# When the expert weights of blocks 1 to 4 are spread out: one number in the order of a hybrid layer

## The chip, the cores and the metric

One core of a Trainium2 chip runs the whole kernel. The metric is the device time of one execution in microseconds (us). A core has engines that work side by side, each in the order of its own instruction list: TensorE (PE in the profile, its weight loads PEld), VectorE (DVE), ScalarE (ACT), GpSimd (POOL), and SyncE (SP), which issues most transfers. Sixteen DMA engines move the data; the transfers that SP, ACT and POOL issue share them.

## The reference, cut to what matters

One layer over 1024 tokens of 1024 numbers (float32). A mixing part (an RWKV-7 recurrence and a latent attention, both gated) is added to x. Then comes PEER, a choice among 16384 experts, and then a gated embedding and a norm:

```
x  += (sigmoid(gate_A) * yA + sigmoid(gate_B) * yB) @ W_out
h2  = rms_norm(x)
# PEER: 8 heads x 16 experts = 128 (index, gate) pairs per token
top_s, top_i = top_k(h2 @ w_q against two sets of 128 keys, 16)   # per head
idx, gate    = the 16 best of the 256 pairs, softmax of their scores
act = gelu(sum_d h2[t, d] * u_tab[idx[t, k], d])                  # 128 dots per token
x  += sum_k gate[t, k] * act[t, k] * v_tab[idx[t, k]]
x  += sigmoid(rms_norm(x) @ W_pg) * (p @ W_ple)
out = rms_norm(x)
```

## The kernel before, in words

The 1024 tokens are eight blocks of 128, and two blocks are a slice (0 to 3). For each slice there is a projection, the recurrence (`rwkv`), the rest of the projection, attention (`attend`), and the choice (`select`): `select` joins the two branches, adds them to x, computes the queries, multiplies them with the keys, and `combine` makes 128 indices and gates for each token of a block.

PEER then has two ways for the sum over v:

- **Dots, all blocks** (`gather`): for each of a block's 128 columns, POOL issues an indirect DMA (L907) that fetches one row of u for each of the 128 tokens (128 rows of 4 KB), and VectorE multiplies it with h2 and sums (L909). Four row buffers are there, seven after `more_rows`. At the end the gates are multiplied by gelu of the dots.
- **Blocks 5, 6, 7** (`add_rows`): the same with rows of v (L922), which VectorE scales and adds to x (L924).
- **Blocks 0 to 4** (`expand`, `dense`): the gates are spread into a full table W, 16384 experts by 128 tokens, and all of v is multiplied with it. `expand_block` splits each index into its upper and lower seven bits, transposes both and the gates, and makes for each token two columns: `oa` (VectorE, L966: where iota equals the upper part, the gate) and `ob` (ScalarE, L961 and L962). TensorE multiplies them (L968), four tokens to a bank of PSUM; ScalarE copies the bank to `ws` (L969); after 64 tokens, half a block, SP issues four writes of 1 MB to W in DRAM (L971). `dense` reads W (L989) and v (L999), splits each number into two parts for a faster matmul form (L282 on ScalarE, L284 on VectorE) and runs 3840 matmuls (L1003 to L1005) for the five blocks together, adding into x by L1008. It can't begin before every block of W is written.

At last `ple` does the gated embedding and the final norm, block by block in the order 0 to 7.

The order on the engines is made by a planner when the kernel is built. Each call in `everything` carries a number; every instruction traced in that call gets it as its priority. The planner follows a modelled time and gives an idle engine, of the instructions that are ready and whose buffers are free, the one with the lowest number. The order so found is fixed: on the chip each engine takes its list in order and waits where an operand is not there yet. So a number does not say when a call runs, only who goes first where two are ready. The part of the list that matters here:

```
(11.2, self.project_rwkv, 3), (10.5, self.attend, 2), (11, self.select, 2), (51, self.gather, [4]),
(49, self.expand, [0]), (16.1, self.rwkv, 3), (15, self.project_rest, 3), (49.5, self.attend, 3), (52.5, self.select, 3),
(52, self.gather, [5]), (49, self.expand, [1, 2, 3, 4]), (60, self.ple_weights, 0), (53, self.more_rows, None),
(53, self.gather, [6, 7]), (50, self.dense, 0),
(56, self.add_rows, 5), (57, self.add_rows, 6), (58, self.add_rows, 7),
(60, self.ple, range(8)),
```

Memory follows the order of the calls as they are written: `expand` of 1 to 4 has its buffers on the right side, where those of `rwkv` 3 lay before, so it can start when that is done. `attend` 3 and `select` 3 lie on the left side. The buffers of `dense` and the three more row buffers lie where theirs and the streamed weights' lay.

Of the kernel before, what the change touches and what calls it, by code (L numbers as in the profile page):

```python
# [151 lines left out]
class Program:  # L152
# [912 lines left out]
    def everything(self):  # L1065
        nc = self.nc
        order = [
            (0, self.project_rwkv, 0), (0.1, self.rwkv, 0), (0.2, self.project_rest, 0), (1, self.attend, 0),
            (1.5, self.select, 0), (50, self.gather, [0, 1]), (2, self.project_rwkv, 1), 
            (4.9, self.rwkv, 1), (5, self.project_rest, 1), (5.2, self.project_rwkv, 2), (5.5, self.attend, 1), (6, self.select, 1),  # L1070
            (50, self.gather, [2, 3]),
            (11.1, self.rwkv, 2), (10, self.project_rest, 2), 
            (11.2, self.project_rwkv, 3), (10.5, self.attend, 2), (11, self.select, 2), (51, self.gather, [4]),
            (49, self.expand, [0]), (16.1, self.rwkv, 3), (15, self.project_rest, 3), (49.5, self.attend, 3), (52.5, self.select, 3),
            (52, self.gather, [5]), (49, self.expand, [1, 2, 3, 4]), (60, self.ple_weights, 0), (53, self.more_rows, None),
            (53, self.gather, [6, 7]), (50, self.dense, 0),
            (56, self.add_rows, 5), (57, self.add_rows, 6), (58, self.add_rows, 7),
            (60, self.ple, range(8)),
        ]
        with ExitStack() as st:  # L1080
            self.kp = self.pool(self.ctx, "cx", "right")
            self.wp = self.pool(st, "wts", "left")
            begun = {}
            self.tc.cur_priority = PHASE // 20
            self.rope_tables()
            for prio, f, a in order:
                if f == self.more_rows:
                    st.close()
                    self.xp = self.pool(self.ctx, "dx", "left")
                    self.gp2 = self.pool(self.ctx, "rows", "left")  # L1090
                    continue
                self.tc.cur_priority = int(prio * PHASE)
                self.aux = nc.gpsimd if f == self.rwkv else nc.vector
                if f == self.project_rwkv:
                    begun[a] = f(a)
                elif f == self.attend:
                    f(a)
                    if a + 1 in begun:
                        begun[a + 1][1].close()
                elif f == self.project_rest:  # L1100
                    begun[a][1].close()
                    f(a, begun[a])
                elif f == self.ple_weights:
                    f("right")
                else:
                    f(a)
# [15 lines left out]
```

## Time and profile before

| what | value |
|---|---|
| median of 3 runs | 3807.69 us (3803.22 to 3827.1) |
| the profiled execution | 3820.92 us, its span 3819.2 us |
| mean granted clock of TensorE in it | 0.886 |
| VectorE, TensorE busy over the span | 81%, 81% |
| moved by DMA | 1160.34 MB, mean 304 GB/s |

Times in the profile count from the span's start. A row of the view of stretches gives the stretch and its length, then the busy time of each engine with its number of instructions, the granted clock of TensorE (1.00 is full), the DMA engines' mean share, and GB/s; asked for one line alone, it has that line's engines only. A row of a timeline gives start, duration, engine, line, operation, output and inputs, the count of like ones merged, and in brackets the idle time before it with what ended it. A row of waits has who waited for whom, the total, how often, and the longest. A row of the chain of work that ended last gives start, duration and what it was.

### The profile page before, as it was taken

To read this page: it belongs to the slowest core of one execution; us is meant where nothing else is said; L and a number is where in the kernel's file an instruction comes from. 1 tells how busy PE (TensorE), PEld (TensorE's weight loads), DVE (VectorE), ACT (ScalarE), POOL (GpSimd) and SP (SyncE) were. 2 spreads that over 40 slices of the span, in tenths; PEclk is the share of its full clock that TensorE was granted. 3 is DMA by queue.
4 is the path that set the end of the run, shared out by engine and by line. 5 is a ranking of instruction groups with operands and counts; after the bars stand their busy time and mean duration, and the time that the engine had idled before them with its cause. 6 is when DMAs were issued, how large, how long until landed. Compare 5 with 4: busy or idle time off the path is not lost. (4 is left out here: it accounts for less than half of the span.)

```text
span 3819.2 us, 60838 instructions
## 1 busy us (share of the span) xinstructions
PE 3111.7 (81%) x21423; PEld 2470.6 (65%) x21423; DVE 3089.1 (81%) x6864; ACT 1299.5 (34%) x2821; POOL 1869.7 (49%) x1502
## 2 busy tenths in 40 slices
PE   6998688768999886698966787737889889888988
PEld 6885677656588774467843566636767667776743
DVE  4632689766789777789978877989999999999996
ACT  4432322124122148311226866642222222222244
POOL 2210355555433543454455433326767766666674
PEclk9998889779999898698977788858999999999999
DMA  6335498889887998998998999889999999999995
GB/s 206 98 92 176 134 342 308 287 300 335 314 290 275 321 334 268 306 355 299 339 290 282 298 336 322 276 305 369 374 384 376 383 374 379 376 367 384 363 331 208
DMA packets 494705, 1160.34 MB, mean 304 GB/s; under 512 B 47680, under 2 KB 222016, under 8 KB 494400
## 3 DMA queue, kind: packets, MB, share of 16 engines
q0 software_dynamic: 202752, 738.29, 53.7%
q1 hardware_dynamic: 274368, 402.42, 30.7%
q10 hardware_dynamic: 17280, 15.74, 1.2%
q8 instruction: 170, 2.79, 0.3%
q14 instruction: 135, 1.11, 0.1%
HBM read 1071.33 MB, written 84.93 MB: 303 GB/s over the span
## 5 line engine op out<-in xcount | busy, mean ns | idle before, releaser
L907 POOL DMA_INDIRECT u<-in_u_dram,idx x1024 | 1229.2, 1200 | 1307.9 <-DVE dots L909 686.9
L909 DVE CUSTOM_DVE_ANT_0 u<-u,gh 128x1024 f32<-128x1024 f32 x1024 | 1243.4, 1225 | 240.6 <-DMA u<-in_u_dram,idx 230.5
L922 POOL DMA_INDIRECT u<-in_v_dram,idx x384 | 496.0, 1292 | 230.0 <-DVE x L924 115.7
L1004 PE MATMUL acc<-vlo,Whi 128*128 128x512 f32 x1280 | 522.3, 408 | 69.2 <-DVE vlo L284 68.5
L1005 PE MATMUL acc<-vhi,Wlo 128*128 128x512 f32 x1280 | 514.4, 402 | 0.0
L1003 PE MATMUL acc<-vhi,Whi 128*128 128x512 f32 x1280 | 369.4, 401 | 95.8 <-DMA vr<-in_v_dram 42.2
L292 PE MATMUL mm<-hT,w 128*128 128x128 f32 x3456 | 418.6, 282 | 3.2 <-ACT z L332 1.7
L292 PEld LDWEIGHTS mm<-hT,w 128*128 128x128 f32 x3456 | 408.6, 197 | 16.4 <-issue 6.0
L1003 PEld LDWEIGHTS acc<-vhi,Whi 128*128 128x128 f32 x1280 | 243.7, 192 | 171.0 <-ACT vhi L282 87.0
L1004 PEld LDWEIGHTS acc<-vlo,Whi 128*128 128x128 f32 x1280 | 249.3, 195 | 146.9 <-DVE vlo L284 95.9
L292 PE MATMUL mm<-act,w 128*128 128x256 f32 x1280 | 315.7, 403 | 28.8 <-DVE gate L779 11.9
L282 ACT ACTIVATE vhi<-vr 128x512 fp32r<-128x512 f32 x256 | 158.0, 628 | 521.6 <-DMA vr<-in_v_dram 378.6
L924 DVE SCALAR_TENSOR_TENSOR x<-u,gate,x 128x1024 f32<-128x1024 f32 x256 | 328.1, 1282 | 6.5 <-DMA u<-in_v_dram,idx 2.3
L968 PE MATMUL w<-ob,oa 128*128 128x128 f32 x1280 | 224.2, 336 | 94.3 <-ACT ob L962 52.6
L292 PEld LDWEIGHTS mm<-act,w 128*128 128x128 f32 x1280 | 252.1, 202 | 70.2 <-DVE gate L779 13.5
L1005 PEld LDWEIGHTS acc<-vhi,Wlo 128*128 128x128 f32 x1280 | 249.7, 195 | 51.6
L968 PEld LDWEIGHTS w<-ob,oa 128*128 128x128 f32 x1280 | 205.4, 243 | 117.6 <-ACT ob L962 79.8
L966 DVE TENSOR_SCALAR oa<-cst,pt 128x128 f32<-128x128 f32 x640 | 186.8, 353 | 40.4 <-PE w L968 37.2
L961 ACT ACTIVATE ob<-cst,pt 128x128 f32<-128x128 f32 x640 | 204.0, 392 | 1.2 <-PE w L968 1.1
L284 POOL TENSOR_TENSOR wlo<-w,whi 128x1024 fp32r<-128x1024 f32 x26 | 63.8, 2452 | 257.5 <-ACT whi L282 239.2
L282 ACT ACTIVATE Whi<-wr 128x1280 fp32r<-128x1280 f32 x64 | 81.5, 1273 | 317.7 <-PE acc L1004 268.3
L284 DVE TENSOR_TENSOR vlo<-vr,vhi 128x512 fp32r<-128x512 f32 x256 | 171.9, 685 | 2.8 <-ACT vhi L282 2.6
(308 smaller groups left out, 5259.3 us busy)
## 6 DMA issues: line engine op xcount, KB each, us to landing
w<-in_w_in_dram SPq DMA_DIRECT2D x144, 512.0 KB
vr<-in_v_dram SPq DMA_DIRECT2D x256, 256.0 KB
W<-ws SPq DMA_DIRECT2D x40, 1024.0 KB
wr<-W SPq DMA_DIRECT2D x64, 640.0 KB
w<-in_w_q_dram SPq DMA_DIRECT2D x64, 512.0 KB
w<-in_w_out_dram SPq DMA_DIRECT2D x32, 512.0 KB
u<-in_u_dram,idx POOLq DMA_INDIRECT x1024, 7.1
x<-in_x_dram SPq DMA_DIRECT2D x16, 512.0 KB
```

The costliest lines, as they stand in the source:

```text
L282: self.nc.scalar.activation(act[0], x, AF.Copy)
L284: (lo_engine or self.aux).tensor_tensor(act[1], x, act[0], op=OP.subtract)
L292: mm(ps, w[0][:, i], a[0][:, i], start=first, stop=last)
L907: nc.gpsimd.indirect_dma_start(out=u[:], out_offset=None, in_=self.I["u"], in_offset=bass.IndirectOffsetOnAxis(ap=idx[:, k:k + 1], axis=0))
L909: nc.vector.tensor_tensor_reduce(out=u[:], in0=u[:], in1=h[:], scale=1.0, scalar=0.0, op0=OP.mult, op1=OP.add, accum_out=dots[:, k:k + 1])
L922: nc.gpsimd.indirect_dma_start(out=v[:], out_offset=None, in_=self.I["v"], in_offset=bass.IndirectOffsetOnAxis(ap=idx[:, k:k + 1], axis=0))
L924: nc.vector.scalar_tensor_tensor(x, v, gate[:, k:k + 1], x, op0=OP.mult, op1=OP.add)
L961: nc.scalar.activation(c[:, i], self.c("iota"), AF.Abs, bias=pt[:, 1, k + i:k + i + 1])
L968: nc.tensor.matmul(ps[:, i], a, c[:, i], start=True, stop=True)
L1003: nc.tensor.matmul(acc[b], wh, vh, start=i == 0, stop=False)
L1004: nc.tensor.matmul(acc[b], wh, vl, start=False, stop=False)
L1005: nc.tensor.matmul(acc[b], wl, vh, start=False, stop=i == G - 1)
```

## The change

One number in the order. The call that expands blocks 1 to 4 had 49, lower than attention 3, the gathers of blocks 4 and 5 and choice 3; it gets 52.8, higher than those and lower than the 53 of the gathers of blocks 6 and 7. The expansion of block 0 and the dense product keep theirs.

```
-            (52, self.gather, [5]), (49, self.expand, [1, 2, 3, 4]), (60, self.ple_weights, 0), (53, self.more_rows, None),
+            (52, self.gather, [5]), (52.8, self.expand, [1, 2, 3, 4]), (60, self.ple_weights, 0), (53, self.more_rows, None),
```

## The prediction

> **What bounds the kernel now.** First the page: span and shares.
>
> ```profile
> span 3819.2 us, 60838 instructions
> PE 3111.7 (81%) x21423; PEld 2470.6 (65%) x21423; DVE 3089.1 (81%) x6864; ACT 1299.5 (34%) x2821; POOL 1869.7 (49%) x1502
> ```
>
> No engine is full over the whole span, so the stages have to be taken apart. The view by stretches does that (busy us of PE, PEld, DVE, ACT, POOL, each with its count; then granted clock, DMA share, GB/s):
>
> ```profile
> 2050.00:2460.00 410.00, 309.33 (x1572) 247.26 (x1571) 334.58 (x1000) 287.34 (x757) 165.32 (x144) 0.84 0.92 309
> 2460.00:2530.00 70.00, 43.73 (x184) 38.01 (x184) 69.90 (x293) 53.22 (x135) 19.16 (x17) 0.59 0.78 259
> 2560.00:3640.00 1080.00, 940.10 (x3840) 735.39 (x3840) 1015.20 (x1299) 241.10 (x330) 725.08 (x548) 0.96 0.99 374
> 3640.00:3819.00 179.00, 154.12 (x400) 67.82 (x400) 145.09 (x209) 73.33 (x154) 101.52 (x78) 0.94 0.74 265
> ```
>
> From 2050 to 2530 three things share the engines: attention and choice of the last slice, the expansion of blocks 1 to 4, and the gathers of blocks 4 and 5. VectorE is busy 82% and then 100%, the DMA 92% and then 78%. From 2560 to 3640 the dense product runs beside the gathers of blocks 6 and 7 and the added rows; VectorE has 94%, the DMA 99%. After 3640 the output stage fills TensorE. Where that stage hands over is read from the timelines of SP, PE, POOL and DVE:
>
> ```profile
> 2111.38 17.66 SPq L971 DMA_DIRECT2D W<-ws  x4
> ...
> 2483.94 15.83 SPq L971 DMA_DIRECT2D W<-ws  x4
> ...
> 2530.51 18.63 SPq L971 DMA_DIRECT2D W<-ws  x4
> 2564.56 0.81 SPq L989 DMA_DIRECT2D wr<-W  x2
> ...
> 2572.08 2.50 PE L1003 MATMUL acc<-vhi,Whi 128*128 128x512 f32 x5 [42.23 <-DMA vr<-in_v_dram]
> ...
> 2585.39 0.20 DVE L876 CAST idx<-idf 128x64 int32<-128x64 f32 x1
> 2587.00 1.68 POOL L907 DMA_INDIRECT u<-in_u_dram,idx  x1 [28.15 <-DVE dots L909]
> ...
> 3643.44 0.66 PE L254 MATMUL tr<-cst,p 128*128 128x128 f32 x2 [8.57 <-DMA p<-in_p_dram]
> ...
> 3781.80 1.28 DVE L924 SCALAR_TENSOR_TENSOR gh<-u,gate,gh 128x1024 f32<-128x1024 f32 x1
> ```
>
> Two chains meet at the end. **The TensorE chain**: the last half block of the expansion is written from 2530.5, read back at 2564.6, the dense product starts at 2572.1 and ends at 3643.4 - 8.6 = 3634.9 (1063 us), and the output stage takes 3643.4 to 3819.2 = 176 us, of which TensorE works 154. **The row chain**: block 7's indices are ready at 2585.6, the last row is added at 3783.1, and 36 us later the last block is out. Both are late together: cutting one alone brings almost nothing, delaying either one costs.
>
> **The change part by part.** Only a number changes, 49 to 52.8. Nothing is added or removed: the same 640 columns (512 of them here), the same 32 writes of W. What the scheduler chose first on each engine, the expansion, now comes behind attention 3 (49.5), the dots of blocks 4 and 5 (51, 52) and choice 3 (52.5); the gathers of 6 and 7 (53) stay behind it. The dense product (50) still can't start before the last W is written. So the question is when the expansion ends.
>
> *What it needs.* The view of stretches, for each of its lines alone (columns made on DVE; then its three ACT steps):
>
> ```profile
> 2050.00:2530.00 480.00, 149.53 (x512) 0.80 0.90 301
> 2050.00:2530.00 480.00, 162.58 (x511) 0.80 0.90 301
> 2050.00:2530.00 480.00, 76.76 (x128) 0.80 0.90 301
> 2050.00:2530.00 480.00, 75.08 (x128) 0.80 0.90 301
> ```
>
> ScalarE needs 163 + 77 + 75 = 314 us, VectorE 150, of 480. At the front it takes (2530.5 - 2111.4) / 7 = 59.9 us per half block; the last half, when the choice's matmuls are over, takes 2530.5 - 2483.9 = 46.6.
>
> *Its pace when it is behind.* Block 0's expansion shows it: that call (49) stood behind attention 2 (10.5), and it ran in that stage's gaps:
>
> ```profile
> 1457.79 16.29 SPq L971 DMA_DIRECT2D W<-ws  x4
> ...
> 1527.49 16.73 SPq L971 DMA_DIRECT2D W<-ws  x4
> ```
>
> That is 69.7 us per half. So "behind" doesn't mean "after": ACT is free enough to be filled.
>
> *How long it is behind.* The choice's product with the keys, in stretches of 20 us, first and last of slice 2 (no expansion beside it) and of slice 3:
>
> ```profile
> 1680.00:1700.00 20.00, 1.22 (x8) 1.21 (x8) 0.90 0.94 337
> ...
> 1760.00:1780.00 20.00, 0.71 (x4) 0.52 (x4) 0.81 0.75 235
> ...
> 2340.00:2360.00 20.00, 0.61 (x4) 0.60 (x4) 1.00 0.97 324
> ...
> 2440.00:2460.00 20.00, 3.91 (x16) 3.38 (x16) 0.70 0.60 178
> ```
>
> That is some 80 us against 120. SP is the queue that both share: a half block's four writes hold it for 14 to 18 us, and loads wait in order behind them:
>
> ```profile
> 2420.52 16.99 SPq L971 DMA_DIRECT2D W<-ws  x4
> 2437.61 9.85 SPq L817 DMA_DIRECT2D keys<-in_keys_dram  x4
> ...
> POOL u L907 <- DVE dots L909: 124.5, 48, 13.4
> POOL u L907 <- DVE oa L966: 110.3, 66, 9.4
> ```
>
> My estimate is that the choice ends at 2400 instead of 2460 (40 us for the key loop, 20 for SP). Until then 350 us / 70 = 5.0 halves; the other 3.0 at 50 us (46.6, and a little for the rows of block 6 beside them) end at 2550: **20 us later** than 2530. Bounds: all eight at 69.7 gives 2608 (+78); on the other side VectorE did 335 + 70 us of work in 480, so without a gap the same work could be through 75 us earlier (-75). I take +20 because the nearest row, block 0, is a filler beside the same kind of stage.
>
> *What is queued behind.* On VectorE a column of the expansion now stands behind dots that wait for their row; the matmuls of L968, the copies on ACT and the writes on SP wait with it. The call's small steps (index split, three transposes, their copies, once a block) move along; on POOL it issues nothing. The eight times four writes cost nothing after the choice, because then SP has only the load of one block of h and the dense product's loads, which need them anyway; if a load of the choice is still behind them, that is 17 us each time. In exchange the rows no longer wait 110 us behind columns (the POOL row above). Their rate (L907 alone, count in brackets):
>
> ```profile
> 700.00:800.00 100.00, 56.13 (x45) 0.74 0.82 281
> 2133.00:2515.00 382.00, 144.72 (x125) 0.82 0.92 311
> ```
>
> 33 rows per 100 us there, 45 where no expansion runs. At 45, block 5 takes 284 us instead of 382 and ends at 2417. Block 6 starts then and not at 2531; by a dense start of 2592 some 75 rows are through. Before, it was 14 when the product began (first and last of 14 rows), and 78 of the 640 stood behind its end:
>
> ```profile
> 2531.19 1.44 POOL L907 DMA_INDIRECT u<-in_u_dram,idx  x1 [17.14 <-DVE idx L876]
> ...
> 2557.91 0.94 POOL L907 DMA_INDIRECT u<-in_u_dram,idx  x1 [0.30 <-issue]
> ...
> 3640.00:3780.00 140.00, 101.52 (x78) 0.96 0.93 331
> ...
> 3801.98 6.98 PE mm L292 x16
> ```
>
> So 640 - 14 - 78 = 548 rows went beside 1063 us of product, 1.94 us each; the lead of 61 rows is worth about 118 us on the row chain.
>
> *What is late next.* That lead is hidden by the TensorE chain: of 565 rows still to come at 2592, 548 fit beside the product as they do now, so its 1063 us stay. It ends at 3655, and the output stage then waits for next to no added row. Of its 176 us TensorE idles 22; 10 stand behind the last matmul (3801.98 + 6.98, the chain's last row above), of the rest I take 8. **Sum: +20 - 8 = +12 us.**
>
> The profiled execution took 3820.9 (span 3819.2), 13 above the median of 3807.7 (3803 to 3827). The difference is put on the median: **3820 us**.
>
> **The rivals.**
> 1. *The rows set the pace of the dense product (faster).* For it: DMA 0.99 at 374 GB/s throughout. 61 rows of 128 x 4 KB are 32 MB, 86 us at that rate. If that bandwidth passes to the loads of v and W, the product shortens by it: 20 - 8 - 86 = -74, **3734**; half of it gives **3777**. TensorE has room: two matmuls of a full run start 0.23 us apart, 3840 x 0.23 = 883 of 1063 us.
>
> ```profile
> 2580.04 0.39 PE L1004 MATMUL acc<-vlo,Whi 128*128 128x512 f32 x1
> 2580.27 0.39 PE L1005 MATMUL acc<-vhi,Wlo 128*128 128x512 f32 x1
> ...
> ACT vhi L282 <- DMA vr<-in_v_dram: 378.6, 132, 9.6
> PE acc L1004 <- DVE vlo L284: 65.3, 51, 3.4
> ```
>
>    Against it: TensorE itself waits for VectorE (65 us), and as long as rows remain, POOL takes up what is freed. Chance 0.20. The Trainium skill ("DMA: Bandwidth & Descriptors", Specifications) puts HBM at about 358 GB/s per core; the 374 here lies a little above, and by that rule the stage is full and this rival is the case. The same page (Measured) has 425 GB/s for one core with its neighbour idle; by that one it is not full. No run here tells the two apart yet.
> 2. *The columns starve behind dots (slower).* Dots whose rows are late hold VectorE in order. If a half takes 90 us until 2400, 3.9 are done, 4.1 x 50 follow: 2605, +75 - 8 = +67, **3875**. It decides from a pace of about 78 us per half on. Against it: columns need 150 of 480 us. Chance 0.26.
> 3. *Really last (slower).* All eight halves after the choice, at 46.6: 2400 + 373 = 2773, +243 - 8: **4043**. Block 0 speaks against it. Chance 0.03.
> 4. *It does nothing.* The gaps were already what the expansion ran in, the order hardly moves: **3808**, give or take 10. Chance 0.08.
>
> **How the numbers follow.** The forecast has 0.43; its own range, from -10 to +45, is the uncertainty of the choice's end and of 50 us per half. The range 3765 to 3885 takes in forecast, rival 4, most of rival 2 and the nearer part of rival 1; about 0.19 is left out. One per cent, 38 us, is about what a measurement of this kernel can tell from none. Faster by more: rival 1 and a little of the forecast, 0.22. Slower by more: rivals 2 and 3 and the edge of the forecast, 0.31. Within: 0.47.
>
> **What would show it.** Right: W's last writes near 2550 and the first dense matmul near 2590; keys done near 2400; block 6's rows beginning some 100 us before the dense product; the dense product still about 1060 us; the last added row well before 3783 while TensorE is full from the end of the dense product to the end. Wrong: a dense product clearly under 1030 us (rival 1), W's last writes after 2590 (rivals 2, 3) or before 2520; or an added row that is still last.

## The result, and the profile after

| kernel | median | runs |
|---|---|---|
| before, same chip | 3809.31 us | 4 |
| after | 3854.89 us (3847.81 to 3856.91) | 4 |

The ratio is 1.0108, 95% interval 1.0085 to 1.0131: slower by about 1%. The profiled execution of after took 3856.91 us, its span is 3855.1; against the span before, 3819.2, that is +35.9. The medians are 46 apart; the pieces below are those of the two profiled executions. Forecast was +12.

First the page's span, and the view by stretches (PE, PEld, DVE, ACT, POOL, then granted clock, DMA share, GB/s) of the kernel after:

```profile
span 3855.1 us, 60828 instructions
...
2050.00:2460.00 410.00, 306.40 (x1508) 242.72 (x1507) 344.57 (x1040) 271.24 (x702) 174.70 (x153) 0.82 0.93 312
2460.00:2530.00 70.00, 41.19 (x185) 36.77 (x186) 66.73 (x285) 55.88 (x144) 16.50 (x17) 0.62 0.85 289
2530.00:2600.00 70.00, 20.61 (x72) 15.98 (x71) 64.20 (x148) 21.67 (x52) 44.61 (x34) 0.52 0.93 319
2600.00:3675.00 1075.00, 934.80 (x3811) 732.29 (x3812) 995.55 (x1241) 236.87 (x323) 709.97 (x542) 0.95 0.98 372
3675.00:3855.00 180.00, 157.85 (x430) 72.42 (x428) 123.65 (x196) 76.76 (x162) 67.73 (x57) 0.96 0.56 203
```

There is a new stretch, 2530 to 2600, in which TensorE does 21 us of 70: the dense product would have begun here, but W isn't complete. Up to 2460 ScalarE did less than before (271 us against 287) and VectorE more (345 against 335). At the other end the output stage has 57 rows beside it, not 78. The handovers, from the timelines of SP, PE, POOL and DVE:

```profile
2344.07 16.64 SPq L971 DMA_DIRECT2D W<-ws  x4
2461.17 24.12 SPq L971 DMA_DIRECT2D W<-ws  x4
2510.95 19.09 SPq L971 DMA_DIRECT2D W<-ws  x4
2566.87 17.05 SPq L971 DMA_DIRECT2D W<-ws  x3
...
2604.73 0.81 SPq L989 DMA_DIRECT2D wr<-W  x2
...
2612.17 2.50 PE L1003 MATMUL acc<-vhi,Whi 128*128 128x512 f32 x5 [45.96 <-DMA vr<-in_v_dram]
...
2508.35 1.44 POOL L907 DMA_INDIRECT u<-in_u_dram,idx  x1 [12.59 <-DVE idx L876]
...
3689.19 0.66 PE L254 MATMUL tr<-cst,p 128*128 128x128 f32 x2 [7.43 <-DMA p<-in_p_dram]
...
3780.64 1.27 DVE L924 SCALAR_TENSOR_TENSOR gh<-u,gate,gh 128x1024 f32<-128x1024 f32 x1
```

Piece by piece along the TensorE chain:

| piece | before | after | difference |
|---|---|---|---|
| dense product starts | 2572.1 | 2612.2 | **+40.1** |
| dense product, its length | 1062.8 | 1069.6 | +6.8 |
| gap to the output stage | 8.6 | 7.4 | -1.1 |
| output stage | 175.8 | 165.9 | **-9.9** |
| span | 3819.2 | 3855.1 | +35.9 |

So the loss is the late start of the dense product. The fifth half block is written from 2344.07, as before (2344.73); the sixth from 2461.17 instead of 2420.52, 117 us after the fifth and not 76; the last from 2566.87 instead of 2530.51. The columns of the expansion alone (L966 on VectorE) show the place, first of the kernel before, then of the one after:

```profile
2050.00:2340.00 290.00, 93.11 (x319) 0.81 0.92 311
2340.00:2400.00 60.00, 13.96 (x49) 0.94 0.94 322
2400.00:2460.00 60.00, 15.49 (x52) 0.86 0.86 281
2460.00:2530.00 70.00, 26.96 (x92) 0.59 0.78 259
```

```profile
2050.00:2340.00 290.00, 94.25 (x324) 0.82 0.94 316
2340.00:2400.00 60.00, 7.87 (x25) 0.94 0.99 347
2400.00:2460.00 60.00, 10.99 (x35) 0.75 0.80 256
2460.00:2530.00 70.00, 27.32 (x94) 0.62 0.85 289
2530.00:2600.00 70.00, 10.51 (x34) 0.52 0.93 319
```

For 290 us the number in the order changed next to nothing in the columns done: 319 and 324. In the 120 us around the choice's product with the keys (its key loop) there are 60 columns where there were 101. Those 41 are missing; 7 more in the stretches around it make up for a part, and 34 come behind 2530. What took their place, by VectorE's groups between 2340 and 2460 (count | busy us, mean ns | idle before), before and after:

```profile
L909 DVE CUSTOM_DVE_ANT_0 u<-u,gh 128x1024 f32<-128x1024 f32 x41 | 49.4, 1213 | 3.1 <-DMA u<-in_u_dram,idx 3.1
L966 DVE TENSOR_SCALAR oa<-cst,pt 128x128 f32<-128x128 f32 x101 | 29.5, 350 | 7.0 <-PE w L968 6.9
L832 DVE FIND_INDEX8 ti<-ts,s 128x8 uint32<-128x128 f32 x28 | 7.7, 284 | 0.0
```

```profile
L909 DVE CUSTOM_DVE_ANT_0 u<-u,gh 128x1024 f32<-128x1024 f32 x48 | 57.9, 1210 | 0.1
L966 DVE TENSOR_SCALAR oa<-cst,pt 128x128 f32<-128x128 f32 x60 | 18.9, 355 | 4.7 <-PE w L968 4.5
...
L832 DVE FIND_INDEX8 ti<-ts,s 128x8 uint32<-128x128 f32 x32 | 8.8, 284 | 0.0
```

Seven more dots and the rest of the choice's searches (32 of each of the five kinds, L831 to L835, where there were 24 to 30) stand for 41 columns, which are 10.6 us of VectorE. VectorE was busy 104 of these 120 us before and 110 after, so it is not its time that ran out. What changed is its list. Counted in the order of its instructions in the trace, 118 columns stand between the choice's first and last search (L831 to L835) in the kernel before, and 50 in the kernel after; the dots between them are nearly as many, 44 and 40. The columns that stood among the searches went behind them. At 2460 the expansion is 36 columns behind (420 done before, 384 after), some 26 us at 46.6 us per half block; the rest then goes a little slower, 52 us per half, and the last column is 38 us late (2527.1 and 2565.1). The waits in the same stretch, before and after:

```profile
PE w L968 <- ACT ob L962: 4.7, 2, 3.2
```

```profile
PE w L968 <- DVE oa L966: 19.9, 9, 9.9
```

Before, the matmuls of the expansion waited in this stretch now and then for ScalarE's columns and never for VectorE's. After, they waited for VectorE's, up to 9.9 us at a time (and 6.2 us in all for ScalarE's). ScalarE was busy 72 us of these 120 before and 52 after, so it wasn't short of time. That the columns which came late held up the four-token steps behind them is read from these lists and waits; no kernel changed VectorE's list alone.

### The profile page after: what moved, and what is told of

Read it like the earlier page. It is cut to its first block, busy times and chain, and to the rows that moved or that the text cites. A ratio compares the mean times of both kernels' runs of the same rounds, so it can differ in the third digit from the quotient of the medians.

```text
span 3855.1 us, 60828 instructions
## 1 busy us (share of the span) xinstructions
PE 3106.8 (81%) x21423; PEld 2468.7 (64%) x21423; DVE 3093.8 (80%) x6864; ACT 1302.2 (34%) x2821; POOL 1852.4 (48%) x1502
## 4 chain that ended last, share of the span: by engine, by line
PE 23%; issue 23%; DVE 21%; DMA 15%; POOL 12%; ACT 4%; SPq 1%; POOLq 0%; DVEq 0%; ACTq 0%
DMA u<-in_u_dram,idx 9%; POOL u L907 8%; DVE u L909 8%; PE mm L292 8%; POOL u L922 3%; DVE oa L966 2%; PE mm L788 2%; PE acc L1004 2%; PE acc L1005 1%; PE w L968 1%; PE acc L1003 1%; PE inv L589 1%; PE mm L294 1%; PE S L738 1%; PE mm L295 1%
## 5 line engine op out<-in xcount | busy, mean ns | idle before, releaser
L907 POOL DMA_INDIRECT u<-in_u_dram,idx x1024 | 1221.4, 1193 | 1320.8 <-DVE dots L909 669.3
L922 POOL DMA_INDIRECT u<-in_v_dram,idx x384 | 486.5, 1267 | 238.5 <-DVE x L924 114.2
L968 PE MATMUL w<-ob,oa 128*128 128x128 f32 x1280 | 241.0, 348 | 132.8 <-DVE oa L966 65.1
L968 PEld LDWEIGHTS w<-ob,oa 128*128 128x128 f32 x1280 | 216.1, 251 | 163.5 <-ACT ob L962 85.2
L966 DVE TENSOR_SCALAR oa<-cst,pt 128x128 f32<-128x128 f32 x640 | 188.4, 354 | 43.1 <-PE w L968 41.0
```

What stands on the lines that cost most here:

```text
L907: nc.gpsimd.indirect_dma_start(out=u[:], out_offset=None, in_=self.I["u"], in_offset=bass.IndirectOffsetOnAxis(ap=idx[:, k:k + 1], axis=0))
L922: nc.gpsimd.indirect_dma_start(out=v[:], out_offset=None, in_=self.I["v"], in_offset=bass.IndirectOffsetOnAxis(ap=idx[:, k:k + 1], axis=0))
L966: nc.vector.tensor_scalar(a, self.c("iota"), pt[:, 0, k:k + 1], pt[:, 2, k:k + 1], op0=OP.is_equal, op1=OP.mult)
L968: nc.tensor.matmul(ps[:, i], a, c[:, i], start=True, stop=True)
```

## The experiments

In the first three sections **theory A** is: to be behind the choice, in its key loop, costs the expansion the 41 columns. **Rivals**: being behind the dots of block 5; or a loss wherever it is behind anything. In the two sections on rows, theory A and its rival are about another question, the prediction's first rival: do the rows set the dense product's length?

### Behind the dots of block 5 only

```
-            (52, self.gather, [5]), (49, self.expand, [1, 2, 3, 4]),
+            (52, self.gather, [5]), (52.3, self.expand, [1, 2, 3, 4]),
```

> The expansion of blocks 1 to 4 at 52.3: behind attention 3 and the dots of blocks 4 and 5, still in front of choice 3 (52.5). Theory A, the choice's key loop is what takes VectorE from the expansion: then nothing is lost here, 3809 give or take 12, W's last writes near 2530 as before. Theory B, the dots of block 5 are what starves the columns: most of the 46 us are lost here, 3840 to 3860, W's last writes near 2570.

Measured: 3824.2 us beside 3816.22, ratio 1.0018 (1.0002 to 1.0034). SP's and PE's timelines:

```profile
2418.68 17.26 SPq L971 DMA_DIRECT2D W<-ws  x4
...
2566.82 2.50 PE L1003 MATMUL acc<-vhi,Whi 128*128 128x512 f32 x5 [39.76 <-DMA vr<-in_v_dram]
```

The sixth half is as early as before (2420.52), the dense product starts 5 us earlier. To stand behind attention and both blocks' dots costs the start nothing. The time lies 3 us above theory A's range, beside a kernel before that took 3816 here and not 3809; theory B's 3840 is far off.

### The choice first, everything else as before

```
-  (49.5, self.attend, 3), (52.5, self.select, 3),
+  (49.5, self.attend, 3), (48.9, self.select, 3),
```

> The expansion stays at 49, choice 3 goes from 52.5 to 48.9: the choice alone passes in front of it (and of the dots of blocks 4 and 5). Theory A (the choice's key loop takes VectorE from the expansion): the dense product starts 25 to 45 us later than before, near 2600 to 2615, and the time is 3835 to 3860. Theory B (the dots do it): the dense product starts where it did, 2572, and the time is 3795 to 3815.

Measured: 3846.76, ratio 1.0082 (1.0057 to 1.0107).

```profile
2457.68 16.00 SPq L971 DMA_DIRECT2D W<-ws  x4
...
2598.46 2.50 PE L1003 MATMUL acc<-vhi,Whi 128*128 128x512 f32 x5 [44.63 <-ACT vhi L282]
```

Here the dots stay behind the expansion and the choice is ahead of it (48.9 is also ahead of attention 3 and of the dots, so theirs is not quite the old place), and the sixth half is 37 us late, the dense product 26. The choice suffices for most of the loss; behind attention and the dots alone the start is not late.

### Blocks 1 and 2 behind, or blocks 3 and 4, or block 4 alone

```
             for b in blocks:
+                self.tc.cur_priority = int((52.8 if 0 < b < 3 else 49) * PHASE) + 5000 * b
                 self.expand_block(b, pool, psum, len(blocks) > 1)
```

with `0 < b < 3`, `b > 2` and `b == 4` for the three.

> Only blocks 1 and 2 of the expansion at 52.8, blocks 3 and 4 at 49. Theory A, the loss is all made in the last three halves, when the key loop runs: 3809 give or take 12, as before. Rival, the loss is spread evenly over the eight halves: 3825 to 3840.

> Blocks 1 and 2 at 49, blocks 3 and 4 of the expansion at 52.8. Theory A, the loss is all made in the last three halves: the full loss, 3845 to 3860, the dense product starting near 2610. Rival, the loss is spread evenly: 3825 to 3840.

> Blocks 1, 2 and 3 of the expansion ahead of the choice as in the kernel before, block 4 alone behind it. Theory A (only the halves that are still to be done in the choice's key loop, 2340 to 2460, lose): the sixth half, block 3's second, keeps its place and its writes start near 2420 as before, block 4's first half loses the 20 to 40 us of the key loop that are left: 3815 to 3835, W's last writes between 2530 and 2555. Rival (what counts is that the last block of the expansion lies behind the choice, wherever it is then): the full loss, 3845 to 3860.

| behind the choice | median | ratio |
|---|---|---|
| blocks 1, 2 | 3805.33 | 0.9974 (0.9953 to 0.9996) |
| blocks 3, 4 | 3854.77 | 1.0105 (1.0080 to 1.0130) |
| block 4 | 3824.41 | 1.0020 (1.0000 to 1.0040) |

The kernel before took 3816.22 beside the first two and 3817.87 beside the third. SP's and PE's timelines of the kernels with blocks 1 and 2, with 3 and 4, and with 4 behind:

```profile
2508.71 11.50 SPq L971 DMA_DIRECT2D W<-ws  x4
...
2539.76 2.50 PE L1003 MATMUL acc<-vhi,Whi 128*128 128x512 f32 x5 [31.70 <-ACT vhi L282]
```

```profile
2461.69 23.21 SPq L971 DMA_DIRECT2D W<-ws  x4
...
2609.58 2.50 PE L1003 MATMUL acc<-vhi,Whi 128*128 128x512 f32 x5 [45.95 <-ACT vhi L282]
```

```profile
2414.11 17.21 SPq L971 DMA_DIRECT2D W<-ws  x4
2486.82 14.25 SPq L971 DMA_DIRECT2D W<-ws  x4
...
2578.73 2.50 PE L1003 MATMUL acc<-vhi,Whi 128*128 128x512 f32 x5 [44.54 <-ACT vhi L282]
```

All three times are in theory A's ranges. Blocks 3 and 4 carry the whole of the loss, with the sixth half (block 3's second) at 2461.69 as in the kernel after. With block 4 alone behind, the sixth half keeps its place, the seventh is 3 us late and the start 7. So it matters which halves stand behind, those that are due in the key loop; and a block 4 that comes behind the choice when that is nearly over loses little.

The kernel with blocks 1 and 2 behind was a little faster than the kernel before. It was run once more:

> The same kernel as first_two_behind (blocks 1 and 2 behind the choice, 3 and 4 ahead of it), with more rounds, since its gain (0.9974) is small. If the gain is the earlier end of W (dense product from 2540 instead of 2572, with both chains ending 18 us earlier in the profile): 3795 to 3810 and a ratio of 0.995 to 0.999. If it was chance: 1.000 within 0.002.

Measured: 3811.27 beside 3817.87, ratio 0.9978 (0.9959 to 0.9997). The small gain is there twice, but it is well under the 1% that the prediction takes as what a measurement of this kernel can tell from none. Its dense product starts 32 and 24 us before that of the kernel before, but lasts 14 and 18 us longer in its two profiles. Why its W is complete earlier wasn't settled.

### Fewer rows beside the dense product

Block 7's dots for 64 of 128 columns, in the kernels before and after:

```
-            for k in range(128):
+            for k in range(64 if b == 7 else 128):
```

With it one small VectorE instruction in every block's `gather` sets the second half of `dots` to zero.

> The kernel before, but block 7's dots are taken for 64 of its 128 columns only; the other 64 dots are set to zero. That leaves out 64 fetched rows of u (64 x 0.52 MB) and their products, all of which lie beside the dense product. It measures how much the rows set the dense product's length. Theory A (TensorE's own chain sets the product; the rows only fill the transfers beside it): the product stays within 20 us of 1063, and the time is 3790 to 3815, the little gain being the output stage that no longer waits for the last blocks. Rival B (the transfers set it; 64 x 0.52 MB at 374 GB/s are 90 us): the product shrinks to 970 to 990, and the time is 3720 to 3745. In between, in proportion.

> The same removal of 64 columns of block 7's dots (64 rows of u left out), on the changed kernel, whose dense product starts 40 us later. Theory A: 3835 to 3855, the distance to the same removal on the kernel before stays at 35 to 45 us, since the late start of the dense product is passed on whole. Rival B (transfers set the pace): 3765 to 3790 with a distance that may be smaller, since the rows that the changed kernel has fetched ahead count there.

Measured: 3784.45, ratio 0.9928 (0.9903 to 0.9953), and 3838.47, ratio 1.0075 (1.0054 to 1.0097). The first lies 6 us below theory A's range, the second in it; both are far from the rival. But the profile shows that the edit was no test of it. The view by stretches of the first one, for its dense product and its output stage:

```profile
2545.00:3614.00 1069.00, 943.97 (x3840) 738.65 (x3839) 1010.40 (x1236) 236.15 (x323) 714.03 (x542) 0.95 0.99 372
3614.00:3788.00 174.00, 151.19 (x400) 67.29 (x400) 89.40 (x166) 76.05 (x161) 31.72 (x27) 0.95 0.33 121
```

POOL issued 542 rows beside 1069 us of product; before, 546 beside 1063. The rows of v moved up, and most of the 64 are missing from the output stage (27 rows, not 78). So the transfers beside the product were never fewer. The 30 us gained are for the most part another thing: the dense product started at 2545, 27 us earlier. The row fetches that were left out lie behind that start, but seven of the eight small instructions that set the dots to zero lie ahead of it, and the planner found another order: VectorE's list differs otherwise too from 2135 us on, and 136 columns stand among the choice's searches where 118 stood. In the two kernels with 64 rows less the starts are 50 us apart and the times 54, more than the 35 to 45 that theory A expected.

The start also varies with no change of the order. In the kernel before and the two kernels of the next section the lists of VectorE, ScalarE and GpSimd are the same up to 3318 us, and the dense product starts at 2572, 2560 and 2561; in the two profiles of the kernel with blocks 1 and 2 behind it starts at 2540 and 2548. So a difference of some 12 us between single profiles says nothing, and the verdict on the choice rests on all kernels together. In the four in which blocks 3 and 4 stand behind the choice (after, choice first, blocks 3 and 4 behind, and after with 64 rows less) 47 to 56 columns stand among its searches, and the dense product starts between 2595 and 2612. In the other nine it is 93 to 136 columns, and a start between 2535 and 2579.

### No rows in the last third of the dense product

The kernel before; blocks 6 and 7 add 8 of 128 rows of v, once with neither fetch nor addition of the rest, once with all additions but no fetch:

```
             for k in range(128):
+                if b > 5 and k >= 8:
+                    break
```

```
             for k in range(128):
-                v = self.row(); (indirect fetch of the row)
+                if b == 5 or k < 8:
+                    v = self.row(); (indirect fetch of the row)
```

> The kernel before, but blocks 6 and 7 add only 8 of their 128 rows of v: 240 rows are neither fetched nor added. So the last third of the dense product (from about 3300) has no rows beside it, which the removal of 64 rows of u did not bring: there the rows behind them moved up, 542 instead of 546 beside the product. In 200 us of the product there are now 720 to 764 matmuls. Theory A (TensorE's own chain, rows only fill): the same 720 to 770 in the stretches without rows, and 3795 to 3810 in all. Rival (rows take from the product, by transfers or by VectorE): 850 or more in those stretches, the product 40 to 60 us shorter, 3740 to 3770 in all.

> The same 240 rows of v are not fetched, but VectorE still does all 240 additions (with a row that is already there), 1.27 us each. It separates what the rows take: if their transfers do, the product's pace in the stretches without fetches rises as in the kernel that has neither (850 or more matmuls in 200 us), and the time is within 15 us of that one. If VectorE's additions do, the pace stays at 720 to 770 while they run, and the time is 3790 to 3815.

Measured: 3754.59, ratio 0.9847 (0.9815 to 0.9880), and 3811.68, ratio 0.9998 (0.9979 to 1.0018). One stretch of 220 us well inside the product, of the kernel before, then without fetch and addition, then with the additions alone:

```profile
3340.00:3560.00 220.00, 195.57 (x813) 153.50 (x813) 213.18 (x216) 48.82 (x67) 145.00 (x115) 0.98 0.99 375
```

```profile
3340.00:3560.00 220.00, 220.00 (x973) 182.16 (x972) 89.16 (x120) 58.21 (x80) 0.00 (x0) 1.00 0.36 117
```

```profile
3340.00:3560.00 220.00, 207.67 (x907) 169.00 (x906) 220.00 (x231) 54.97 (x75) 0.00 (x0) 1.00 0.35 110
```

Without rows TensorE is busy for the whole 220 us and does 973 matmuls, 20% more than the 813 beside rows (0.226 us each against 0.271; the granted clock, 1.00 against 0.98, can be 2% of it). With the transfers gone and VectorE still full it does 907. So of the 160 matmuls that the rows cost, 94 come back when the transfers go and 66 more when the additions go too; fetches without additions were not run, so the shares hold for this order only. Theory A in its strict form, that rows only fill, is wrong: they slow the product. The whole product took 1030 and 1046 us instead of 1063: 33 us less without rows, where the rival had said 40 to 60. The second kernel's total, 3811.68, is no faster because the additions reach into the output stage, which lasts 199 us instead of 176: from 3600 to 3700 VectorE is busy 99 us and TensorE 72. The Trainium skill ("DMA: Bandwidth & Descriptors", Specifications) puts HBM at about 358 GB/s per core; by that a stretch at 375 is full and transfers set its pace. The trace agrees in part: at 110 GB/s the pace rose by 12%, and VectorE, busy all 220 us, held it from there. That the stretch was full at 375 is not shown by it.

### The writes of W from two queues

```
-                nc.sync.dma_start(self.W[part][q]...
+                (nc.scalar if q % 2 else nc.sync).dma_start(self.W[part][q]...
```

in the kernel before, and in the one with blocks 1 and 2 behind.

> The kernel before, with the four writes of each half block of W issued in turn by SyncE and ScalarE instead of all by SyncE. It measures whether the holding of SyncE's queue by the writes (14 to 19 us for four, 78.8 us for eight in the changed kernel) is a part of the way from the last column of W (2526.8) to the first read (2564.6). If it is: the dense product starts 5 to 12 us earlier and the time is 3803 to 3812. If only the landing of the writes counts: 3812 to 3822, no difference. If ScalarE, which has the matmuls' splits and the copies of the banks, is held by its issues: 3820 to 3840.

> Blocks 1 and 2 behind the choice, blocks 3 and 4 ahead as in the kernel before (3805 in its own run, dense product from 2540 instead of 2572), and in addition the writes of W issued in turn by SyncE and ScalarE. If both gains are real and independent: 3790 to 3800. If the issue of the writes doesn't matter: 3800 to 3810. If ScalarE is held by them: above 3812.

Measured: 3847.43, ratio 1.0102 (1.0074 to 1.0130), and 3841.49, ratio 1.0083 (1.0062 to 1.0104): the first above all three of its ranges, the second in its third, ScalarE held by the issues. The view by stretches of the first one, for its dense product and its output stage:

```profile
2548.00:3607.00 1059.00, 936.63 (x3840) 733.37 (x3840) 1004.01 (x1365) 235.87 (x324) 712.73 (x536) 0.96 0.98 373
3607.00:3838.00 231.00, 153.86 (x400) 67.89 (x400) 192.33 (x251) 76.13 (x161) 138.81 (x113) 0.85 0.79 286
```

Its dense product starts 24 us earlier and ends 28 us earlier, and still the kernel is slower: the output stage lasts 231 us, in which TensorE works 154, as before. It waits for rows: 113 are issued in that stretch, where 78 were, and TensorE waits 54 us at one place for a block that VectorE hands on when its last row is added (L1039). This is the row chain of the prediction, alone at the end. Fifteen of the rows were lost far ahead, ten more beside the product (536 issued, not 546); L907 on POOL between 2050 and 2340, before and with two queues:

```profile
2050.00:2340.00 290.00, 122.48 (x104) 0.81 0.92 311
```

```profile
2050.00:2340.00 290.00, 103.01 (x89) 0.81 0.85 285
```

Why 15 rows fewer are fetched there, with the DMA engines at 0.85, stays open. In that stretch the expansion's matmuls waited 51 us for ScalarE's columns instead of 29, and VectorE's columns 39 us for those matmuls instead of 22, which fits a ScalarE that is held by its issues. But the planned order had changed too, VectorE's from 1475 us on, and no run separates the two. (The expectation's 78.8 us for eight writes is one merged row, with the wait for the last columns in it.)

## Why the prediction was right and wrong

The direction of the sum and its two chains were right, its main term was half of what came.

- **The choice ends at 2400 instead of 2460: this step failed.** The first and last matmuls of the key product (L820), of slice 3 before and after:

```profile
2355.86 0.61 PE L820 MATMUL tr<-keys,gate 128*128 128x128 f32 x4
2453.48 0.71 PE L820 MATMUL tr<-keys,gate 128*128 128x128 f32 x4 [0.49 <-ACT s L822]
```

```profile
2354.84 0.61 PE L820 MATMUL tr<-keys,gate 128*128 128x128 f32 x4
2427.49 1.06 PE L820 MATMUL tr<-keys,gate 128*128 128x128 f32 x4
```

  The end came 26 us earlier, not 60, and block 6's indices at 2507.9, 23 us earlier. Slice 2 was the right row to go by: its key product took from 1691.6 to 1761.5, 70 us, and slice 3's 74 after, 98 before. But the 80 and the 120 were counted differently from the rows of 20 us: 80 is from the first row's start to the last row's start, 120 from the first row's start to the last row's end. Counted alike they are 100 and 120, 20 us apart and not 40. The other 20 us, for SP, did not come on top. With an end of 2434 the prediction's own rates give 5.5 halves and then 2.5 at 50 us, 2560: +30 instead of +20.
- **5.0 halves until 2400 at 70 us, then 3.0 at 50: the rate was the wrong kind of number.** At 2400 there were 324 + 25 = 349 columns, 5.5 halves, more than assumed. Up to 2340 the expansion kept its old rate; in the 120 us around the key loop it fell to 60 columns, 128 us per half. A mean rate of block 0 behind another slice can't show that: the loss sits in the one stretch where the choice's searches now stand first in VectorE's list. After 2460 the last 128 columns took 105 us, 52 per half: that 50 was right. Together the last matmuls of the expansion come at 2566 and the dense product at 2612.2, +40 where +20 was said. The expansion did not catch up what it lost.
- **Starving behind dots (rival 2)**: the columns did starve, but behind the choice; to be behind the dots cost 0.2%. Its condition, more than 78 us per half until 2400, was not met: it was 64 until then, and 128 only around the key loop.
- **The rows run at 45 per 100 us once they don't wait for columns: this step failed too, at little cost.** In the stretch in which the prediction counted 125 rows there are 130, and POOL still waited for columns, 105 us where it was 83:

```profile
2133.00:2515.00 382.00, 146.92 (x130) 0.81 0.91 309
...
POOL u L907 <- DVE oa L966: 105.0, 50, 10.8
```

  Block 5's last row was issued at 2494.8, 18 us earlier than before, and not at 2417. Block 6's rows then waited for its indices and began at 2508.35. That this is 104 us before the dense product, where some 100 was said, is luck: the prediction's own 2417 and 2592 would be 175 us. POOL issued 42 rows until 2612, not 75, a lead of 28 and not 61. The sum took this lead for hidden, so it lost little by it.
- **The product stays 1063 us: it held**, at 1069.6; in the profiles of the kernels that leave the rows whole it lies between 1058 and 1084, a spread that no edit explains. The reason given against rival 1, that POOL takes up what is freed, was what the run with fewer rows showed (542 against 546). But "rows set the pace" is no empty rival: in the stretch with no rows the product is 20% faster. By that a lead would help once rows run out before the product does; no run had such a lead.
- **The output stage gains 8: right**, 9.9, of which 6.8 are idle time of TensorE (14.8 us instead of 21.6) and 3 its own work (151.1 us instead of 154.1). The sign given for it was not seen as it was put: the last row is added at 3781.9, hardly earlier, but 73 us before the end instead of 36.
- **Sum**: +40 + 7 - 1 - 10 = +36, against +20 + 0 + 0 - 8. The mis-sized term is the start of the dense product: the last writes of W begin 36 us later, not 20, and the way from there to the first read took 4 more.

## What to carry to other kernels

A scheduler's number changes the order only where two things are ready at once: find the stretches in which the work that now goes first competes for an engine (here 120 of 480 us) and price the change there, not with a mean rate. The list itself can be counted in a trace; here the columns among the choice's searches told the kernels with a late start from the others better than any single time. Before counting on work that starts earlier, check that what you move is what holds it: the rows still waited for columns, and then for their indices. When two lengths are read from rows of a view, count both from the same ends. And where two chains end together, a gain on one is no gain: the two queues brought the product's end forward by 28 us and lost 1%.

## What the runs showed of the hardware that was not expected

- The four writes of a half block, 1 MB each, held SP's queue 24, 19 and 23 us for the last three halves of the kernel after (2566.87 to 2589.7 for the last), against 17, 16 and 19 before. The first read of W comes 38 us after the last half's first write, 34 before: 4 of the 40 us.
- The dense product's matmuls, at 0.271 us each beside rows, took 0.226 us with TensorE busy throughout and a granted clock of 1.00, in a stretch with transfers at 117 GB/s and VectorE busy 89 of 220 us.
